# A decoder layer on one Trainium2 core: its forms of x at one place modulo 256 bytes

## Chip, core and metric

The chip is a Trainium2 (trn2). The kernel runs on one of its cores, and the metric is the device time of one execution in microseconds (us). A core has five engines that run their own instruction streams and wait for one another by semaphores: TensorE (PE), which multiplies a stationary operand, loaded first (PEld), with a moving one that streams past it; VectorE (DVE), ScalarE (ACT), GpSimd (POOL) and SyncE (SP), which here issues most DMAs. Operands lie in the on-chip memory SBUF, 128 partitions with byte addresses of their own; matmul results accumulate in PSUM.

## What is computed

One layer that joins two recurrent branches over 16 meta rows and 512 sequence rows of width 1024: retention (4 heads) and gated linear attention, "the linear branch" (4 heads). All arithmetic is float32.

```python
def hybrid_layer(h, norm_gain, w_in, w_gate_up, b_gate, ret_norm_gain, gla_norm_gain,
                 w_branch_ret, w_branch_gla, w_out):
    u = rms_norm(h, norm_gain)
    proj = u @ w_in
    (rq, rk, rv, rg, gq, gk, gv, gg, glr, m_ret, m_gla) = jnp.split(proj, points, axis=-1)
    ...
    o_ret = retention_chunked(rq, rk, rv)
    o_ret = head_group_norm(o_ret, ...) * jax.nn.silu(rg)
    ...
    o_gla = gla_chunked(gq, gk, gv, log_a)
    o_gla = head_rms_norm(o_gla, ...) * jax.nn.silu(gg)
    merged = jax.nn.sigmoid(m_ret) * (o_ret @ w_branch_ret) + jax.nn.sigmoid(m_gla) * (o_gla @ w_branch_gla)
    return h + merged @ w_out
```

The output is the final RMS norm of the 512 sequence rows.

## The kernel before

**Numbers in two parts.** A float32 operand is kept as hi + lo, both in the type fp32r: ACT casts hi, DVE subtracts it to give lo (`split`, L154, for weights; `form`, L684 to L690, for x). A product of two operands is three matmuls: hi by hi, hi by lo, lo by hi (`mm3` at L189, L192 and L193, and L318).

**Block products.** Most projections are done by `quad` (L257 to L396). It takes a 2x2 block matrix of x (two halves of the rows by two halves of the 1024 columns of the input, transposed) and a block of 2x256 weight columns, and needs seven block products instead of eight, on seven *forms*: the blocks A11, A12 and A22 and the combinations S1 to S4 of blocks. The order is A11 (product 1), A12 (2), S2 (6), S3 (7), S1 (5), A22 (4), S4 (3), or with `early` 1, 7, 6, 2, 5, 4, 3. One product (`product`, L302 to L319) is 2 column tiles by 4 k-blocks by 3 matmuls: 24 matmuls of a 128x128 stationary tile and 256 moving columns. With `wide` (gqk, rqk: queries and keys) the moving side has 264 columns, except for S1 and S4, where it has 256. With `rows=True` (gg, gv, rg, rv: gates and values of the linear branch and of retention; wo1: a part of the output projection) the form is stationary and the weight moves. Otherwise (gqk, rqk; mr, mg: merge gates; bg: projection of the linear branch) the weight is stationary and the form moves. The number behind a name is that of the head or pair of heads. The tiles gg_a, gg_b, gg_c and so on are a quad's three PSUM results.

**Weights.** They are loaded by SP (some with an addition on POOL's DMA), combined on DVE (L355, L356, L372, L379), split (`prepare`) into rotating buffers of hi and lo, and used by one product each. TensorE waits for the lo part where DVE is late.

**Forms.** Those of x are made at the start, from u00, u01 and u11 (parts of the normalised, transposed x), and read by all quads over w_in; the four blocks also by gq0, gk0 and gv0, which use no combinations (L428, L643). The linear branch has its own forms of its output for bg, and the merged rows (mh, ml, with their combinations ms, `merged_sums` L1471) have theirs for wo1; the last 256 columns of the output projection (`wo_p`, "wo2") use the merged rows directly, as stationary operands. Each form is a tile of 4 k-blocks; the stride between k-blocks follows from its width.

**Order.** The stages are generators that `weave` mixes: forget gates (L731 on) and first projections; gg0 with the linear attention; gqk1, gv1, gg1; bg0 and bg1; per head of retention rqk, rg, rv with scores and attention; mg and mr beside the attention of head 3 (`ret_attention`, L1329); the retention's branch product (br); wo. A scheduler of the framework then sets the row of instructions on each engine. A tile with an earlier tile's tag takes its place, and its first writer waits for the last reader of the earlier one. `quad` yields after each product, so that others' small matmuls come between products; `sooner` (gg0 only) prepares the weights of product 6 during product 2. `total` (L826) adds a product's result to the copy of another (gg_x, L334) into gsg, the gate's sum. At L910 to L954 stand small matmuls of the linear attention.

**Tiles in question.** xh0, xl0, xh1, xl1 hold the blocks of x (hi and lo by column half); fh3 to fh6 and fl3 to fl6 hold S1 to S4. o3 (oh, ol of head 3) takes the tags of xh0 and xl0; the first merged rows take xh1 and xl1, and their sums the tags of S1 to S4.

```python
        def product(i, form, w, ps, fresh, ready=None):
            ...
                    u = [row(f[form], kk)[:, col] if rows else row(f[form], kk)[:, :n] for f in forms]
                    v = [f[:, kk, :] if rows else f[:, kk, col] for f in (hi, lo)]
```

Of the kernel before, what the change touches and what calls it, by code (L numbers as in the profile page):

```python
# [21 lines left out]
F32 = mybir.dt.float32  # L22
F32R = mybir.dt.float32r
# [5 lines left out]
P = 128  # L29
D = 1024  # L30
T = 512
NM = 16
TT = T + NM
HT = TT // 2
HM = NM // 2
HW = 272
KD = D // P
NTB = T // P
# [3 lines left out]
C_GQ, C_GK, C_GV, C_GG = 6144, 6656, 7168, 8192  # L42
# [6 lines left out]
A11, A12, A22, S1, S2, S3, S4 = range(7)  # L49
# [59 lines left out]
def hybrid_kernel(ctx: ExitStack, tc: tile.TileContext, I, out: bass.AP):  # L109
    nc = tc.nc  # L110

    cp = ctx.enter_context(tc.tile_pool(name="cp", bufs=1))
# [13 lines left out]
    nc.gpsimd.memset(one, 1.0)  # L126


    xh = [cp.tile([P, 4, 2, HW], F32R, tag=f"xh{i}", name=f"xh{i}") for i in range(2)]
    xl = [cp.tile([P, 4, 2, HW], F32R, tag=f"xl{i}", name=f"xl{i}") for i in range(2)]  # L130
    ah = {(th, kh): xh[kh][:, :, th] for th in range(2) for kh in range(2)}
    al = {(th, kh): xl[kh][:, :, th] for th in range(2) for kh in range(2)}
    fh = [ah[0, 0], ah[0, 1], ah[1, 1]]
    fl = [al[0, 0], al[0, 1], al[1, 1]]
    fh += [cp.tile([P, 4, HW], F32R, tag=f"fh{i}", name=f"fh{i}") for i in range(3, 7)]
    fl += [cp.tile([P, 4, HW], F32R, tag=f"fl{i}", name=f"fl{i}") for i in range(3, 7)]

    rt = cp.tile([P, NTB + 1], F32, name="rt")
    rneg = cp.tile([P, NTB + 1], F32, name="rneg")
# [25 lines left out]
    def act(ins):  # L165
        return queue("act", ins)

    def vec(ins):
        return queue("vec", ins)
# [34 lines left out]
    def weave(dense, chain, skip=0):  # L204

        for n, _ in enumerate(dense):
            tick()
            if n >= skip:
                next(chain, None)
        for _ in chain:  # L210
            pass
# [286 lines left out]
    def meta_rows(psm, name):  # L498
# [9 lines left out]
    xc = ctx.enter_context(tc.tile_pool(name="xc", bufs=2))  # L508
    gctx = ctx.enter_context(ExitStack())
    g1 = gctx.enter_context(tc.tile_pool(name="g1", bufs=1))  # L510
    la = g1.tile([P, 5, 512], F32, name="la")
    gsum = g1.tile([P, 640], F32R, name="gsum")
    gsm = g1.tile([NM, NM], F32R, name="gsm")
    gmask = g1.tile([P, 3, P], I32, name="gmask")
# [8 lines left out]
    gp = gctx.enter_context(tc.tile_pool(name="gp", bufs=1, reuse_waits="tile"))  # L523
# [11 lines left out]
    ss = sp.tile([P, NTB + 1], F32, tag="ss5", name="ss5", bufs=1)  # L535


    xr = [gp.tile([P, D], F32, tag=("gq", "gk", "gX", "gX")[n], name=f"xr{n}", bufs=(1, 1, 2, 2)[n])
          for n in range(NTB)]
    xr.append(laf[:, :D])  # L540
# [3 lines left out]
    for q in range(4):  # L544
        raw = wraw(f"gv0_{q}_w", (P, 2, 512))
        for s in (slice(0, 1), slice(1, 2)) if q < 2 else (slice(0, 2),):
            k0, n = 2 * q + s.start, s.stop - s.start
            x = (nc.sync if k0 else nc.scalar).dma_start(u[k0 // 4][:, k0 % 4:k0 % 4 + n], I["xt"][:, k0:k0 + n])
# [57 lines left out]
    for q in range(4):  # L606
        raw = graw[q]
        hi, lo = wsplit([P, 2, 512], f"gv0_{q}")
        for kk in range(2):
            kh, k = divmod(2 * q + kk, 4)  # L610
# [3 lines left out]
            if k == kh == 0:  # L614
                nc.vector.tensor_copy(hi[:, kk, :], raw[:, kk, :])
                w = nc.vector.tensor_sub(lo[:, kk, :], raw[:, kk, :], hi[:, kk, :].bitcast(F32))
            x = nc.vector.scalar_tensor_tensor(xl[kh][:, k, :, :HT], u[kh][:, k], g, xh[kh][:, k, :, :HT].bitcast(F32),
                                               op0=ALU.mult, op1=ALU.subtract)
# [5 lines left out]
        if q == 3:  # L624
            for kh in range(2):
                for k in range(4):
                    x = nc.scalar.activation(u[kh][:, k], u[kh][:, k], AF.Copy, scale=ng[:, 4 * kh + k:4 * kh + k + 1])
# [54 lines left out]
    vec(nc.vector.scalar_tensor_tensor(u01, u00, -1.0, u01, op0=ALU.mult, op1=ALU.subtract))  # L682

    def form(i, x):  # L684
        act(nc.scalar.copy(fh[i][:, :, :HT], x))

        def rest():
            vec(nc.vector.tensor_sub(fl[i][:, :, :HT], x, fh[i][:, :, :HT].bitcast(F32)))

        return rest  # L690

    forms = [form(S1, u11)]
# [38 lines left out]
    def forget_gates():  # L731
# [22 lines left out]
        parts["gk0", 0] = wsplit([P, 4, 256], "gk0_0")  # L754
        forms.append(form(S2, u00))
        next_weights(0)
        forms.append(form(S4, u01))
        for i in (2, 0, 1, 3):
            forms[i]()
        yield  # L760
        def values(p):
# [78 lines left out]
    G = {}  # L840
# [3 lines left out]
                        lambda psm: meta_v(psm, p), False)  # L844

    def gla_g(p):
        sg = g1.tile([P, NTB, 512], F32, tag="gsg", name=f"gsg{p}")
        G["sg", p] = sg

        def evac(n, th, x, y):  # L850
            total(sg[:, 2 * th:2 * th + 2, n * 256:(n + 1) * 256], x, y)

        yield from quad((C_GG + p * 512, C_GG + p * 512 + 256), True, f"gg{p}", evac,
                        sooner=p == 0)

    def gla_qk(p):
        q = gp.tile([P, 2, T], F32, tag="gq", name=f"gq{p}")
# [404 lines left out]
        yield  # L1262

    def ret_g(h):
        sg = rp.tile([P, NTB, 512], F32, tag="sg", name=f"sg{h}")
        R["sg", h] = sg
        yield from quad((C_RG + h * 512, C_RG + h * 512 + 256), True, f"rg{h}", rows_into(sg, AF.Silu),
                        ahead=h % 3 == 0, behind=R.get(("pow", h - 1)))
# [60 lines left out]
    def ret_attention(h):  # L1329
        sh, sl, sm = R["s", h]  # L1330
        vh, vl = R["v", h]
        vm, sg = R["vm", h], R["sg", h]

        if h == 0:
            nc.gpsimd.memset(rp.tile([P, 16], F32, name="gap"), 0.0)
        oh, ol = [(rp if h < 3 else cp).tile([P, 4, T], F32R, tag=f"o{n}" if h < 3 else f"x{n}0", name=f"o{n}{h}")
                  for n in "hl"]
        R["o", h] = oh, ol

        def values(ib):  # L1340
            ps = pat(f"av{h}{ib}")
            for jb in range(ib + 1):
                o = SOFF[jb] + (ib - jb) * P
                mm3(ps, sh[:, o:o + P], sl[:, o:o + P], vh[:, jb, :], vl[:, jb, :], jb == 0, False)
            nc.tensor.matmul(ps, sm[:, ib * P:(ib + 1) * P], vm, start=False, stop=True)
            b6 = sp.tile([P, 6], F32, tag="b6", name=f"b6{h}{ib}")
            mv = sp.tile([P, 2], F32, tag="mv", name=f"mv{h}{ib}")
            nc.vector.bn_stats(b6, ps)
            nc.vector.bn_aggr(mv, b6)
            r = rstd_of(mv[:, 1:2], 1.0, P, f"g{h}{ib}")  # L1350
            nm = sp.tile([P, 1], F32, tag="nm", name=f"nm{h}{ib}")
            nc.vector.scalar_tensor_tensor(nm, mv[:, 0:1], -1.0, r, op0=ALU.mult, op1=ALU.mult)  # L1352
            on = tmp(f"on{h}{ib}")
            nc.scalar.activation(on, ps, AF.Identity, scale=r, bias=nm)  # L1354
            nc.vector.tensor_mul(sg[:, ib, :], on, sg[:, ib, :])

        for ib in range(NTB):
            values(ib)
            R["pow", h] = R["pow"]
            yield  # L1360
        if h < 2:
            yield
        for half in range(2):
            turn(sg, half, oh, ol, rgain, h * 4, f"ot{h}")
            yield
# [82 lines left out]
    for h in range(4):  # L1448
# [10 lines left out]
        else:  # L1459
            weave(run(ret_g(h), ret_v(h)), run(every(ret_rope(h), 3, 2, at if h else None), ret_scores(h)))  # L1460
    weave(gates_ret(), ret_attention(3))

    mh, ml = [[cp.tile([P, 4, T], F32R, tag=f"x{n}1", name=f"m{n}0"),
               rp.tile([P, 4, T], F32R, tag=("sg", "vl")[n == "l"], name=f"m{n}1")] for n in "hl"]
    sums = [[cp.tile([P, 4, 256], F32R, tag=f"f{n}{i}", name=f"ms{n}{i}") for i in range(3, 7)] for n in "hl"]
    mforms = [[m[0][:, :, :256], m[1][:, :, :256], m[1][:, :, 256:], *x] for m, x in zip((mh, ml), sums)]

    def merged(k, t):
        return [m[k // 4][:, k % 4, t * P:(t + 1) * P] for m in (mh, ml)]
# [30 lines left out]
    def residual():  # L1500
        nc.sync.dma_start(hs[0], I["x"][:, :512].rearrange("(t p) d -> p t d", p=P))
        yield
        nc.sync.dma_start(fgb, I["final_norm_gain"].to_broadcast([P, D]))
        nc.sync.dma_start(hs[1], I["x"][:, 512:].rearrange("(t p) d -> p t d", p=P))

    weave(ret_branches(), residual(), skip=14)

# [104 lines left out]
```

## Time and profile before

| what | us |
|---|---|
| median of 3 runs (lowest to highest) | 758.31 (757.18 to 758.43) |
| the profiled execution's own time | 759.11 |
| its span in the profile | 757.3 |
| granted TensorE clock over the span | 0.998 |
| DMA traffic over the span | 153 GB/s |

The 40 slices of the profile (tenths of a slice in which TensorE is busy) are 9 in all but the last. A row of the *chain of waits* has a start, a time and what the chain was on; the row of `x24` matmuls is one product. In the *timeline* a row has in addition the operation, the output, the inputs and their shapes. In the table of *windows* each engine's busy time has its instructions behind it in brackets. Busy time of one matmul (0.28 us and so on) is a modelled length that overlaps with the next one's; the step from one to the next is read from the chain's rows or from two starts.

### The profile page before, as it was taken

The numbers are of one execution on the slowest core, as the hardware profiler recorded it, in microseconds if no ns is written. First come the engines' busy times: TensorE is split into PE (matmuls) and PEld (weight loads), VectorE is DVE, ScalarE is ACT, GpSimd is POOL, SyncE is SP. The second block draws the span as 40 slices with busy tenths as digits, with TensorE's granted clock in tenths as the row PEclk, the third lists the DMA queues.
The fourth block names the chain that finished last, engine by engine and source line by source line (L and its number), as shares of the span: only waits on it lengthen the run. The fifth ranks groups of instructions, "written<-read, shape, count | busy, mean of one in ns | idle before, by whom it ended". The sixth has DMA issues, their size and how long they took to land.

```text
span 757.3 us, 14065 instructions
## 1 busy us (share of the span) xinstructions
PE 748.2 (99%) x5595; PEld 701.3 (93%) x5595; DVE 609.2 (80%) x873; ACT 450.4 (59%) x764; POOL 138.8 (18%) x173
## 2 busy tenths in 40 slices
PE   9999999999999999999999999999999999999996
PEld 6799899999999999999989999989999999988996
DVE  6699877679897789789957688966787989775994
ACT  7897584666974466556546555646464756532562
POOL 2211110101221122110530100440011210111142
PEclk9999999999999999999999999999999999999999
DMA  9863421821589972733783562795476356687503
GB/s 301 286 141 78 118 63 50 195 85 57 130 182 272 305 165 88 168 112 133 199 249 117 120 159 86 204 223 136 130 166 145 107 144 189 227 194 210 128 29 112
DMA packets 100138, 117.42 MB, mean 155 GB/s; under 512 B 5732, under 2 KB 90852, under 8 KB 99816
## 3 DMA queue, kind: packets, MB, share of 16 engines
q1 hardware_dynamic: 79896, 88.19, 36.7%
q0 software_dynamic: 19888, 27.79, 20.3%
q8 instruction: 44, 0.72, 0.4%
q10 hardware_dynamic: 288, 0.53, 0.2%
q14 instruction: 22, 0.18, 0.1%
HBM read 104.44 MB, written 11.53 MB: 153 GB/s over the span
## 4 chain that ended last, share of the span: by engine, by line
PE 86%; DVE 6%; ACT 2%; DMA 2%; issue 2%; POOL 1%; POOLq 0%; DVEq 0%; ACTq 0%
PE rqk_b L318 6%; PE rv_b L318 6%; PE rg_b L318 6%; PE rqk_c L318 5%; PE br_p L193 3%; PE br_p L189 3%; PE br_p L192 3%; PE gg_b L318 3%; PE gv_p L643 3%; PE mg_b L318 3%; PE rv_c L318 3%; PE rg_c L318 3%; PE mr_b L318 2%; PE bg_b L318 2%; PE gg_c L318 2%
## 5 line engine op out<-in xcount | busy, mean ns | idle before, releaser
L189 PE MATMUL br_p<-oh,br_h 128*128 128x512 f32 x128 | 50.0, 390 | 0.0
L193 PE MATMUL br_p<-oh,br_l 128*128 128x512 f32 x128 | 50.0, 390 | 0.0
L192 PE MATMUL br_p<-ol,br_h 128*128 128x512 f32 x128 | 49.8, 389 | 0.0
L154 ACT CAST rv_h<-rv_w 128x1024 fp32r<-128x1024 f32 x24 | 25.3, 1052 | 27.2 <-DVE rv_w L372 9.6
L154 DVE TENSOR_TENSOR rv_l<-rv_w,rv_h 128x1024 fp32r<-128x1024 f32 x24 | 29.3, 1221 | 9.2 <-ACT rv_h L154 9.2
L154 DVE TENSOR_TENSOR rg_l<-rg_w,rg_h 128x1024 fp32r<-128x1024 f32 x20 | 24.4, 1220 | 8.3 <-ACT rg_h L154 8.3
L154 ACT CAST rg_h<-rg_w 128x1024 fp32r<-128x1024 f32 x20 | 21.0, 1052 | 15.6 <-PE br_p L192 6.0
L282 POOL DMA_DIRECT2D rqk_x<-in_w_in_dram x8 | 10.4, 1302 | 105.4 <-DVE rv_l L154 80.6
L193 PEld LDWEIGHTS br_p<-oh,br_l 128*128 128x128 f32 x128 | 24.0, 188 | 5.2
L192 PEld LDWEIGHTS br_p<-ol,br_h 128*128 128x128 f32 x128 | 24.0, 188 | 4.7
L189 PEld LDWEIGHTS br_p<-oh,br_h 128*128 128x128 f32 x128 | 24.1, 188 | 4.5
L154 ACT CAST rqk_h<-rqk_w 128x1024 fp32r<-128x1024 f32 x20 | 21.1, 1053 | 11.5 <-PE rqk_c L318 2.9
L154 ACT CAST br_h<-br_w 128x1024 fp32r<-128x1024 f32 x16 | 16.8, 1050 | 18.7 <-PE br_p L192 9.5
L154 DVE TENSOR_TENSOR rqk_l<-rqk_w,rqk_h 128x1024 fp32r<-128x1024 f32 x20 | 24.4, 1221 | 3.9 <-ACT rqk_h L154 3.8
L1354 ACT ACTIVATE on<-av,nm,g_r 128x512 f32<-128x512 f32 x16 | 12.5, 779 | 25.3 <-DVE nm L1352 25.3
L318 PE MATMUL rv_b<-rv_l,fh 128*128 128x256 f32 x96 | 27.1, 282 | 0.2 <-DVE rv_l L154 0.2
L318 PE MATMUL rqk_b<-fh,rqk_h 128*128 128x256 f32 (+1 forms) x96 | 27.2, 283 | 0.0
L318 PE MATMUL rqk_b<-fh,rqk_l 128*128 128x256 f32 (+1 forms) x96 | 27.1, 282 | 0.0
L318 PE MATMUL rqk_b<-fl,rqk_h 128*128 128x256 f32 (+1 forms) x96 | 27.1, 282 | 0.0
L318 PE MATMUL rg_b<-rg_h,fl 128*128 128x256 f32 x96 | 27.0, 281 | 0.0
L318 PE MATMUL rv_b<-rv_h,fl 128*128 128x256 f32 x96 | 27.0, 281 | 0.0
L318 PE MATMUL rg_b<-rg_l,fh 128*128 128x256 f32 x96 | 26.9, 280 | 0.0
(721 smaller groups left out, 3260.8 us busy)
## 6 DMA issues: line engine op xcount, KB each, us to landing
rv_w<-in_w_in_dram SPq DMA_DIRECT2D x16, 512.0 KB, 4.2
br_w<-in_w_branch_ret_dram SPq DMA_DIRECT2D x16, 512.0 KB, 3.4
rqk_w<-in_w_in_dram SPq DMA_DIRECT2D x12, 512.0 KB, 4.8
rg_w<-in_w_in_dram SPq DMA_DIRECT2D x12, 512.0 KB, 4.5
rqk_x<-in_w_in_dram SPq DMA_DIRECT2D x8, 512.0 KB, 4.0
rqk_x<-in_w_in_dram POOLq DMA_DIRECT2D x8, 512.0 KB, 8.0
rg_x<-in_w_in_dram SPq DMA_DIRECT2D x8, 512.0 KB, 3.7
rg_x<-in_w_in_dram POOLq DMA_DIRECT2D x8, 512.0 KB, 7.8
```

The costliest lines, as they stand in the source:

```text
L154: return nc.scalar.copy(hi, src), nc.vector.tensor_sub(lo, src, hi.bitcast(F32))
L189: m = nc.tensor.matmul(o, lh, rh, start=first, stop=False)
L192: nc.tensor.matmul(o, lh, rl, start=False, stop=False)
L193: m = nc.tensor.matmul(o, ll, rh, start=False, stop=last)
L282: x = nc.gpsimd.dma_start(t, block(0, 1), accum_op=ALU.add)
L318: m = nc.tensor.matmul(ps[t][:, :n] if wide else ps[t], l, r, start=first and j == 0, stop=kk == 3 and j == 2, skip_group_check=not fresh ...
L643: m = nc.tensor.matmul(pss[t], (al if j == 1 else ah)[t // 2, kh][:, k, c], (lo if j == 2 else hi)[:, kk, :], start=q == kk == j == 0, sto ...
L1354: nc.scalar.activation(on, ps, AF.Identity, scale=r, bias=nm)
```

## The change

The tiles of x and its sums become six: x0, x1 and x2, hi and lo, with 576, 896 and 640 columns per k-block, so that the stride between k-blocks is 2304, 3584 and 2560 bytes, multiples of 256. Unused tiles (`gap`) of 16, 32 or 48 floats shift what follows them in its pool. S1 and S4 keep 256 columns instead of 264. S4 takes the place of a part of the block A(1,0) (second half of the rows, first half of the columns), which no form uses, but which gq0, gk0 and gv0 read; its making moves from the forget gates into `gla_g(0)`, behind the first product of gg0, and the tile sg of that stage is allocated behind it. o3 takes the place of S2 and S3 (x2). Of the sums of merged rows, S1's lies behind the first merged rows in x1, S2's and S3's take x0, and S4's takes o3's place.

Addresses that follow from the allocation, modulo 256 bytes, by k-block where they change:

| operand | before | after |
|---|---|---|
| A11, A12 of x, hi and lo | 192 and 64 in turn | 128 |
| A22 of x | 0 and 128 in turn | 128 |
| S1 to S4 of x | 192, 0, 64, 128 | 128 |
| A(1,0) of x | 0 and 128 in turn | 192 |
| linear branch: A11 | 64 | 128 |
| linear branch: A22 | 0 | 128 |
| linear branch: S3 | hi 0, lo 128 | 128 |
| linear branch: A12, S1, S2, S4 | 128 | 128 |
| merged rows, first half of the columns | 192 | 128 |
| merged rows, second half | hi 64, lo 128 | 128 |
| sums of merged rows | 192 | 128 |
| split weights, hi and lo | 192 | 192 |

The diff, with most unchanged lines left out:

```diff
-    xh = [cp.tile([P, 4, 2, HW], F32R, tag=f"xh{i}", name=f"xh{i}") for i in range(2)]
-    xl = [cp.tile([P, 4, 2, HW], F32R, tag=f"xl{i}", name=f"xl{i}") for i in range(2)]
+    def gap(pool, n, name):
+        pool.tile([P, n], F32, name=name)
+
+    gap(cp, 48, "gap0")
+    x0, x1, x2 = [[cp.tile([P, 4, w], F32R, tag=f"x{n}{i}", name=f"x{n}{i}") for n in "hl"]
+                  for i, w in enumerate((576, 896, 640))]
+    gap(cp, 16, "gap1")
+
+    def halves(t, w):
+        return t[:, :, :2 * w].rearrange("p k (t c) -> p k t c", t=2)
+
+    xh, xl = [[halves(a, HW), halves(b, 320)] for a, b in zip(x0, x1)]
     ah = {(th, kh): xh[kh][:, :, th] for th in range(2) for kh in range(2)}
     al = {(th, kh): xl[kh][:, :, th] for th in range(2) for kh in range(2)}
-    fh = [ah[0, 0], ah[0, 1], ah[1, 1]]
-    fl = [al[0, 0], al[0, 1], al[1, 1]]
-    fh += [cp.tile([P, 4, HW], F32R, tag=f"fh{i}", name=f"fh{i}") for i in range(3, 7)]
-    fl += [cp.tile([P, 4, HW], F32R, tag=f"fl{i}", name=f"fl{i}") for i in range(3, 7)]
+    fh, fl = [[a[0, 0], a[0, 1], a[1, 1], b[:, :, 640:], c[:, :, :320], c[:, :, 320:], z[:, :, 320:]]
+              for a, z, b, c in zip((ah, al), x0, x1, x2)]
...
     g1 = gctx.enter_context(tc.tile_pool(name="g1", bufs=1))
+    gap(g1, 16, "gap2")
     la = g1.tile([P, 5, 512], F32, name="la")
+    gap(g1, 48, "gap3")
     gsum = g1.tile([P, 640], F32R, name="gsum")
...
+    gap(gp, 32, "gap4")
     xr = [gp.tile([P, D], F32, tag=("gq", "gk", "gX", "gX")[n], name=f"xr{n}", bufs=(1, 1, 2, 2)[n])
...
     def form(i, x):
-        act(nc.scalar.copy(fh[i][:, :, :HT], x))
+        w = 256 if i in (S1, S4) else HT
+        h, l, x = fh[i][:, :, :w], fl[i][:, :, :w], x[:, :, :w]
+        act(nc.scalar.copy(h, x))
         def rest():
-            vec(nc.vector.tensor_sub(fl[i][:, :, :HT], x, fh[i][:, :, :HT].bitcast(F32)))
+            vec(nc.vector.tensor_sub(l, x, h.bitcast(F32)))
...
         next_weights(0)
-        forms.append(form(S4, u01))
-        for i in (2, 0, 1, 3):
+        for i in (2, 0, 1):
             forms[i]()
...
     def gla_g(p):
+        def evac(n, th, x, y):
+            total(sg[:, 2 * th:2 * th + 2, n * 256:(n + 1) * 256], x, y)
+
+        products = quad((C_GG + p * 512, C_GG + p * 512 + 256), True, f"gg{p}", evac, sooner=p == 0)
+        if p == 0:
+            next(products)
+            form(S4, u01)()
+            yield
         sg = g1.tile([P, NTB, 512], F32, tag="gsg", name=f"gsg{p}")
         G["sg", p] = sg
-
-        def evac(n, th, x, y):
-            total(sg[:, 2 * th:2 * th + 2, n * 256:(n + 1) * 256], x, y)
-
-        yield from quad((C_GG + p * 512, C_GG + p * 512 + 256), True, f"gg{p}", evac,
-                        sooner=p == 0)
+        yield from products
...
     def ret_g(h):
+        if h == 0:
+            gap(rp, 16, "gap5")
         sg = rp.tile([P, NTB, 512], F32, tag="sg", name=f"sg{h}")
+        if h == 0:
+            gap(rp, 48, "gap6")
         R["sg", h] = sg
...
         if h == 0:
-            nc.gpsimd.memset(rp.tile([P, 16], F32, name="gap"), 0.0)
-        oh, ol = [(rp if h < 3 else cp).tile([P, 4, T], F32R, tag=f"o{n}" if h < 3 else f"x{n}0", name=f"o{n}{h}")
-                  for n in "hl"]
+            gap(rp, 16, "gap7")
+        if h < 3:
+            oh, ol = [rp.tile([P, 4, T], F32R, tag=f"o{n}", name=f"o{n}{h}") for n in "hl"]
+        else:
+            oh, ol = [cp.tile([P, 2560], F32R, tag=f"x{n}2", name=f"o{n}{h}")[:, 16:16 + 4 * T]
+                      .rearrange("p (k c) -> p k c", k=4) for n in "hl"]
         R["o", h] = oh, ol
...
-    mh, ml = [[cp.tile([P, 4, T], F32R, tag=f"x{n}1", name=f"m{n}0"),
-               rp.tile([P, 4, T], F32R, tag=("sg", "vl")[n == "l"], name=f"m{n}1")] for n in "hl"]
-    sums = [[cp.tile([P, 4, 256], F32R, tag=f"f{n}{i}", name=f"ms{n}{i}") for i in range(3, 7)] for n in "hl"]
-    mforms = [[m[0][:, :, :256], m[1][:, :, :256], m[1][:, :, 256:], *x] for m, x in zip((mh, ml), sums)]
+    def rows4(t, o, c):
+        return t[:, o:o + 4 * c].rearrange("p (k c) -> p k c", k=4)
+
+    m0 = [cp.tile([P, 3584], F32R, tag=f"x{n}1", name=f"m{n}0") for n in "hl"]
+    mh, ml = [[rows4(t, 0, T), rp.tile([P, 4, T], F32R, tag=("sg", "vl")[n == "l"], name=f"m{n}1")] for n, t in zip("hl", m0)]
...
     weave(ret_branches(), residual(), skip=14)
+
+    mforms = []
+    for n, m, t in zip("hl", (mh, ml), m0):
+        s23 = cp.tile([P, 2048], F32R, tag=f"x{n}0", name=f"ms{n}0")
+        s4 = cp.tile([P, 1024], F32R, tag=f"x{n}2", name=f"ms{n}2")
+        mforms.append([m[0][:, :, :256], m[1][:, :, :256], m[1][:, :, 256:], rows4(t, 4 * T, 256),
+                       rows4(s23, 0, 256), rows4(s23, 1024, 256), rows4(s4, 0, 256)])
```

On DVE at the start of gg0 the rows stand as follows; xl is S4's lo part, gk_p a product of keys, gg_6_h and gg_6_l the split weights of product 6. Before:

```order
L868 TENSOR_TENSOR gk_441<-gk_p_589,rb 128x264
L868 TENSOR_TENSOR gk_441<-gk_p_591,rb 128x264
L372 TENSOR_TENSOR gg_w_732<-gg_w_732,gg_x_734 128x1024
L379 TENSOR_TENSOR gg_w_733<-gg_w_733,gg_w_732 128x1024
L154 TENSOR_TENSOR gg_6_l<-gg_w_732,gg_6_h 128x1024
L826 TENSOR_TENSOR gsg_731<-gg_a,gg_x_775 128x2x256
L923 TENSOR_TENSOR gK_823<-gX_812,gk_441 128x512
```

And on DVE at the same place of the changed program:

```order
L883 TENSOR_TENSOR gk_440<-gk_p_586,rb 128x264
L883 TENSOR_TENSOR gk_440<-gk_p_588,rb 128x264
L701 TENSOR_TENSOR xl_82<-u_130,xh_81 128x4x256
L380 TENSOR_TENSOR gg_w_728<-gg_w_728,gg_x_730 128x1024
L838 TENSOR_TENSOR gsg_775<-gg_a,gg_x_771 128x2x256
L387 TENSOR_TENSOR gg_w_729<-gg_w_729,gg_w_728 128x1024
L162 TENSOR_TENSOR gg_6_l<-gg_w_728,gg_6_h 128x1024
L938 TENSOR_TENSOR gK_822<-gX_811,gk_440 128x512
```

S4's subtraction has come in ahead of the weights' sums, and the add into gsg now stands ahead of the second weight sum and of gg_6_l, where it stood behind both.

On DVE at the forget gates, where the four combinations were subtracted; fl are the lo parts. Before:

```order
L154 TENSOR_TENSOR gk_0_l<-gk_w_468,gk_0_h 128x1024
L688 TENSOR_TENSOR fl_89<-u_130,fh_85 128x4x264
L688 TENSOR_TENSOR fl_88<-u_131,fh_84 128x4x264
L688 TENSOR_TENSOR fl_90<-u_130,fh_86 128x4x264
L688 TENSOR_TENSOR fl_91<-u_131,fh_87 128x4x264
L791 SCALAR_TENSOR_TENSOR fg_a<-fg_a,fg_e_510 128x512
```

And at the same place of the changed program, where xl are the lo parts:

```order
L162 TENSOR_TENSOR gk_0_l<-gk_w_467,gk_0_h 128x1024
L701 TENSOR_TENSOR xl_86<-u_129,xh_85 128x4x264
L701 TENSOR_TENSOR xl_84<-u_130,xh_83 128x4x256
L701 TENSOR_TENSOR xl_86<-u_129,xh_85 128x4x264
L803 SCALAR_TENSOR_TENSOR fg_a<-fg_a,fg_e_507 128x512
```

Three are left; one of them has 256 columns for 264.

## Prediction

> **What bounds the kernel now.** I read three things in this order: the shares of the page, the chain of work that ended last, and the chain's own rows, where each stretch of 24 matmuls of one product (one `product` call, 128 stationary columns by 256 or 264 moving ones) is one row: start, us, line, count.
>
> ```profile
> span 757.3 us, 14065 instructions
> PE 748.2 (99%) x5595; PEld 701.3 (93%) x5595; DVE 609.2 (80%) x873; ACT 450.4 (59%) x764; POOL 138.8 (18%) x173
> PE 86%; DVE 6%; ACT 2%; DMA 2%; issue 2%; POOL 1%; POOLq 0%; DVEq 0%; ACTq 0%
> ```
>
> The chain is TensorE's for 86%, so a shorter step from one matmul to the next shortens the span nearly everywhere. The next view is the chain from 237 to 294 us, three kinds of block product one behind the other:
>
> ```profile
> 237.12 2.82 PE bg_c L318 x24
> 242.68 2.72 PE bg_a L318 x24
> 245.40 2.72 PE bg_b L318 x24
> 248.12 2.83 PE bg_c L318 x24
> 250.94 2.73 PE bg_b L318 x24
> 253.67 2.93 PE rqk_b L318 x24
> 265.33 2.85 PE rqk_b L318 x24
> 268.18 2.90 PE rqk_c L318 x24
> 273.92 2.85 PE rg_b L318 x24
> 285.30 2.84 PE rg_b L318 x24
> 288.14 2.75 PE rg_c L318 x24
> 290.89 2.85 PE rg_b L318 x24
> ```
>
> All but the two rqk rows of 2.93 and 2.90 (264 columns) are 24 matmuls of 128x256 without a wait. They take 2.72 to 2.85 us, 113 to 119 ns each. What differs is where the operands lie (table in the section on the change). In bg (branch product of the linear branch) the weight is stationary, at 192 modulo 256 bytes in every row; the form moves. The A12, S1 and S4 products (242.68, 245.40, 250.94), with a form constantly at 128, go at 2.72 or 2.73. S3 (237.12), hi at 0 and lo at 128, takes 2.82; A22 (248.12), constantly at 0, takes 2.83. In rg the form is stationary and the weight moves. Forms whose place changes from one k-block to the next take 2.84 or 2.85; A22 (288.14), which alternates between 0 and 128, takes 2.75. So I read the time as one of place: about 2.73 where the form is at 128 against a weight at 192, about 0.1 more elsewhere.
>
> **The change part by part.** (1) *Forms of x to one place.* Nothing is added per product; 24 matmuls stay 24. rg: the seven products of rg0 run from 273.92 to 290.89+2.85 = 293.74, 19.82 us. At 2.73 each they take 19.11: 0.7 per quad. For constant stationary forms at 128 no row exists. The nearest are the A22 row above, half of whose blocks lie at 128 (2.75), and from the other side the slowest row of this shape, of wo1 (2.88, below). I take 2.73 and keep 2.88 for a rival. rqk: its weight is stationary and the seven products run from 253.67 to 273.92, 20.25 us. The two of 256 columns (S1, S4: 265.33 is one) go from 2.85 to 2.73. For five of 264 at a constant place no row exists; between 2.90 (no gain) and 2.73x264/256 = 2.81 I take 2.84. New sum 2x2.73+5x2.84 = 19.66: 0.59 per quad. The merge gates also move the form:
>
> ```profile
> 648.37 2.84 PE mr_c L318 x24
> 654.18 2.84 PE mr_b L318 x24
> ```
>
> 7x(2.82-2.73) = 0.63 per quad, with 2.82 taken as the mean since other rows of mr stand at 2.80. Where TensorE ends last throughout the quad I count it whole: rg0 to rg2 and rv0 to rv2 6x0.7 = 4.2; mg0, mg1 1.26; mr1 0.63; rqk0 to rqk3 2.36; gqk1 0.59 (taken as rqk); gv1 and gg1 1.4. Of gg0 the last five products 0.5, of rv3 the last five 0.5. Nothing from 187 to 231 us, where a load of og and the vector work after it end last. Together 11.44.
>
> (2) *Linear branch's input.* The three rows above 2.73 of bg1 (A11 taken as A22, S3, A22): 3x0.1 = 0.3, estimated from the rows 237.12 and 248.12. bg0 lies before 237 and gets none.
>
> (3) *Merged rows and their sums.* The last rows of the chain, and two matmuls of the last projection with 42 steps between them:
>
> ```profile
> 734.30 2.80 PE wo_c L318 x24
> 737.10 2.88 PE wo_b L318 x24
> 739.81 0.28 PE L189 MATMUL wo_p<-wo_h,mh 128*128 128x256 f32 x1
> 744.78 0.28 PE L189 MATMUL wo_p<-wo_h,mh 128*128 128x256 f32 x1
> ```
>
> 737.10 is S4 of wo1: form stationary, constantly at 192, as the weight is; 2.88, or 120.0 ns each, the slowest rhythm of this shape. 734.30 is A22, at 64 (hi) and 128 (lo): 2.80. Behind them 42 steps take 4.97 us, 118.3 ns, so 72 of them have 72x5 ns = 0.36 over 113.3. At one place of 128 I count 0.3 for the last three products of wo1 and 0.4 for the rest. Sum of (1) to (3): 12.4.
>
> (4) *S4's form moved.* S4 now lies in x's A(1,0), which gq0, gk0 and gv0 still read, so its cast on ACT and subtraction on DVE move from the forget gates to a point inside gg0.
>
> ```profile
> 40.87 2.85 PE gq_p L428 x24
> 61.71 2.86 PE gg_a L318 x24
> 64.57 0.12 PE ge L910
> 65.74 2.86 PE gg_b L318 x24
> 41.21 4.76 DVE L688 TENSOR_TENSOR fl<-u,fh 128x1056 fp32r<-128x1056 f32 x4
> 63.21 1.23 DVE L379 TENSOR_TENSOR gg_w<-gg_w,gg_w 128x1024 f32<-128x1024 f32 x1
> 64.36 1.22 DVE L154 TENSOR_TENSOR gg_l<-gg_w,gg_h 128x1024 fp32r<-128x1024 f32 x1
> 65.49 0.68 DVE L826 TENSOR_TENSOR gsg<-gg_a,gg_x 128x512 f32<-128x512 f32 x1
> ```
>
> The four subtractions take 4.76, 1.19 each; DVE does the same work in all, at another time. But its order changes: the add into gsg, which waits for the end of product 2 (64.57), stood behind gg_l, the low weights of product 6, and now stands ahead of it. Queued behind it on DVE are the 1.23 and 1.22 above; for gg_l TensorE waits. From the end of gg_a to product 6 it was 65.74-64.57 = 1.17, filled by small products. Now it is at least 0.62 (to the next start) + 1.15 + 1.22 = 3.0: 1.8 lost. Against it stand the products from 34 to 64, ten groups of 24 at 0.13 at most (2.86-2.73), 1.3, which nothing else counts. Net 0.5 lost. ACT's cast delays the copy gg_x, which has from 61.71 to 64.57 to be ready: nothing.
>
> (5) *256 columns for S1 and S4*: 8 of 264 columns of four instructions of about 1.2, 0.15 in all, on engines that wait here; the products read 256 before. Nothing.
>
> (6) *o3 in S2's and S3's place, sums of merged rows in three others.* S2 and S3 are last read by mr1's products before 651.21 (648.37+2.84); o3's first write comes later:
>
> ```profile
> 659.14 0.83 ACT L494 ACTIVATE oh<-ot,rgain 128x256 fp32r<-128x256 f32 x2
> 725.99 1.22 ACT L154 CAST msh<-sigr 128x512 fp32r<-128x512 f32 x2 [2.20 <-DVE sigr L1491]
> ```
>
> 8 us of cover. The sum that takes o3's place is the last of the four, written around 726, after the branch products have read o3. If this cover went, the wait would be a part of a product, under 3 us; I count nothing. The memset removed on POOL (18% busy) costs nobody.
>
> (7) *Given back.* In the rows between products and small matmuls the fast rhythm may have to be found again: for some fourteen interruptions between 300 and 664 I take 0.1 each, 1.4, the gain of one product each, an estimate from 2.83-2.73. And DVE is the next bound:
>
> ```profile
> 273.00:295.00 22.00, 22.00 (x203) 21.35 (x205) 22.00 (x29) 16.02 (x24) 8.21 (x4) 1.00 0.37 106
> 586.00:609.00 23.00, 23.00 (x211) 22.26 (x213) 23.00 (x32) 15.95 (x27) 4.93 (x5) 1.00 0.37 115
> 705.00:731.00 26.00, 25.81 (x207) 25.10 (x205) 26.00 (x37) 14.89 (x30) 7.88 (x9) 1.00 0.25 69
> 614.42 1.15 DVE rv_l L154
> 615.62 2.98 PE rv_b L318 x23
> ```
>
> Columns: PE, weight loads, DVE, ACT, POOL busy, clock, DMA share, GB/s. DVE is full to the last 0.01 us in all three. From 586 to 609 and from 705 to 731 the chain goes over to DVE and a faster TensorE only waits longer (rv3's product 6 starts at 615.62 behind rv_l), so rg3, rv3's first two and wo1's first four count for nothing. From 273 to 295 DVE also has work that can wait; I take 1.0 lost there and in rv0 to rv2, between 0 and the 2.1 that rg0 to rg2 bring.
>
> Sum: 12.4-0.5-1.4-1.0 = **9.5 us** off the profiled run's own 759.11 gives 749.6. The shown runs' median, 758.31, lies 0.8 below that run: **748.8**.
>
> [...]
>
> **The rivals.** *(a) Only moving forms gain.* The A22 rows of rg may owe their 2.75 to alternation, not to 128. Then rg, rv, gv1, gg1, gg0 and wo keep their time: of the 12.4 go 4.2+1.4+0.5+0.5+0.7 = 7.3; 5.1 stays, less 0.5 and about half of (7), 1.2: 3.4, **754.9**. For it: no row shows a constant stationary form that is fast. Against it: the 2.88 of S4 in wo1 shows that a stationary form's place matters.
>
> *(b) DVE takes more.* All of 2.1 in rg0 to rg2 and the same in rv0 to rv2 goes to DVE: 4.2 lost instead of 1.0, gain 6.3, **752.0**. Against it: in rg0 the chain stays with TensorE although DVE is full.
>
> *(c) Place does nothing, or the rows' differences come from the data or the order.* Then of the change only (4) is left, between 0.5 (with cover that I don't see) and its full 1.8, midway 1.2: **759.5**. For it, that only one kernel was seen; against it, that bg's rows return to 2.72 wherever the place is 128.
>
> *(d) Slower.* A stationary form at one constant place locks in the slow rhythm, whichever place: S4 of wo1, the only row here with hi and lo constantly at one place, shows 2.88. Ten row quads (rg0 to rg2, rv0 to rv2, gv1, gg1 and most of gg0 and rv3) at 7x2.88 = 20.16 against 19.82 lose 3.4; with (4) without its offset 1.8 and the column products' gain of 5.1 lost to longer waits only in part (2.5 left), 2.7 more than before: **761.0**. It decides when the row products come out above 2.83. For it: that row. Against it: there weight and form share 192, here they don't, and A22 of wo1 (734.30), constant with hi at 64 and lo at 128, takes 2.80.
>
> **How the numbers follow.** Forecast 0.62, (a) 0.17, (b) 0.08, (c) 0.06, (d) 0.07. The forecast's own range: the fast end has nothing of (7) and of (4), 264 columns at 2.81 (25 products at 0.03, 0.75), and also gains 0.1 in each of the thirteen products that I left at nothing under DVE (rg3, two of rv3, four of wo1): 12.4+0.75+1.3 = 14.4, 743.9. Its other end is (b). The range reaches from 744.0 over (a) to 757.0, beyond which lie most of (c) and (d). A measurement of this kernel tells about 0.2%, 1.5 us, from no change. Faster by more: forecast, (a), (b), less a little: 0.85. Within: most of (c) and the ends of (a) and (d): 0.08. Slower by more: (d) and the bad end of (c): 0.07.
>
> **What would show it.** Right: rg and rv rows of 2.72 to 2.75 for all seven products; bg c rows at 2.72; rqk at 2.81 to 2.87 and 2.73; wo_b at 2.73; a gap of about 3 us between gg_a and the next gg_b. Wrong: row products still at 2.84 (a) or above 2.86 (d); the chain going to DVE from 273 to 345 (b); TensorE waiting for o3 or for the merged sums; bg rows as before (c).

## The result, and the profile after

| | median of its runs, us | lowest to highest | ratio to before | 95% interval |
|---|---|---|---|---|
| before | 757.89 (22 runs) | 756.84 to 758.79, one run at 810.82 | | |
| the change | 759.70 (22 runs) | 756.75 to 762.16 | 1.0023 | 1.0013 to 1.0032 |

The change makes the kernel slower by a little; forecast were 748.8 us, with a range of 744 to 757. The runs of the change also spread over 5.4 us, those of before over 2.0 (the one at 810.82 apart). The profiled execution of the change took 760.18 us of its own, with a granted clock of 0.994. Its page:

```profile
span 758.4 us, 14064 instructions
PE 746.5 (98%) x5595; PEld 699.4 (92%) x5595; DVE 608.8 (80%) x873; ACT 450.1 (59%) x764; POOL 138.6 (18%) x172
PE 85%; DVE 7%; ACT 3%; issue 2%; DMA 2%; POOL 1%; POOLq 0%; DVEq 0%; ACTq 0%
```

TensorE's share of the chain is one point lower than before, DVE's and ACT's are one point higher each (rounded). Where that happens is seen by following the same row of work through both chains. gqk_c is the first product of gqk1 that runs without a break. Here are gg0's first matmul (from the timeline) and the row of gqk_c (from the chain), before and, in the second fence, after:

```profile
58.71 0.28 PE L318 MATMUL gg_b<-gg_h,xh 128*128 128x256 f32 x1
106.41 2.92 PE gqk_c L318 x24
```

```profile
57.45 0.28 PE L326 MATMUL gg_b<-gg_h,xh 128*128 128x256 f32 x1
110.51 2.88 PE gqk_c L326 x24
```

The change is 4.1 us late there, although gg0's first matmul started 1.3 us earlier than before. Later it makes good 3.0 of the 4.1: its span is only 758.4-757.3 = 1.1 longer. So there are two questions: what costs 4.1+1.3 = 5.4 us from gg0's start to gqk_c, and why do the 650 us behind it bring 3 and not some 9. For the first, the windows after, then before (us; PE, weight loads, DVE, ACT, POOL busy; granted clock; DMA share; GB/s):

```profile
64.00:66.00 2.00, 0.67 (x4) 0.29 (x2) 2.00 (x3) 1.35 (x3) 0.00 (x0) 1.00 0.00 0
66.00:68.00 2.00, 0.60 (x3) 0.46 (x3) 2.00 (x3) 2.00 (x7) 1.02 (x2) 0.66 0.00 0
68.00:70.00 2.00, 2.00 (x11) 2.00 (x11) 2.00 (x5) 1.48 (x2) 0.00 (x0) 0.50 0.69 196
70.00:72.00 2.00, 2.00 (x12) 2.00 (x11) 1.35 (x2) 0.00 (x0) 0.43 (x1) 0.50 0.19 67
```

```profile
64.00:66.00 2.00, 2.00 (x17) 1.96 (x17) 2.00 (x3) 2.00 (x6) 0.19 (x1) 1.00 0.00 0
66.00:68.00 2.00, 2.00 (x20) 2.00 (x19) 2.00 (x5) 2.00 (x6) 0.45 (x1) 1.00 0.61 175
```

TensorE idles for 2.7 of 4 us while DVE is full, and behind that its granted clock is 0.50: 11 and 12 matmuls in 2 us, where 17 and 20 ran before. The timeline shows what the 2.7 us wait for, the first two matmuls of product 6 (in brackets the idle time before and what ended it):

```profile
65.75 0.39 PE L326 MATMUL gg_b<-gg_h,xh 128*128 128x256 f32 x1 [1.33 <-ACT gg_h L162]
67.54 0.58 PE L326 MATMUL gg_b<-gg_l,xh 128*128 128x256 f32 x1 [1.40 <-DVE gg_l L162]
```

For the second question, rows of the chain after:

```profile
251.38 2.83 PE bg_c L326 x24
254.20 2.83 PE bg_b L326 x24
...
268.56 2.75 PE rqk_b L326 x24
271.30 2.91 PE rqk_c L326 x24
...
276.95 2.72 PE rg_b L326 x24
293.27 2.72 PE rg_b L326 x24
...
300.89 2.83 PE rv_a L326 x24
735.40 2.83 PE wo_c L326 x24
738.23 2.83 PE wo_b L326 x24
```

In all these products the form is at 128 and the weight at 192; rqk_c has 264 columns, the others 256. There are two times for this one shape: 2.72 or 2.83, with little between (2.75 where a product changes over). I call them two *rhythms*: steps of about 113 and 118 ns that hold over a stretch. rg0 is at 2.72 from its first product to its last, rv0 behind it at 2.83, bg1 at 2.83 where it had four rows of 2.72 to 2.74 before.

### The profile page after: what moved, and what is told of

It reads as the page before. It is cut to its first block, busy times and chain, and to the rows that moved or that the text cites. A ratio compares the mean times of both kernels' runs of the same rounds, so it can differ in the third digit from the quotient of the medians.

```text
span 758.4 us, 14064 instructions
## 1 busy us (share of the span) xinstructions
PE 746.5 (98%) x5595; PEld 699.4 (92%) x5595; DVE 608.8 (80%) x873; ACT 450.1 (59%) x764; POOL 138.6 (18%) x172
## 4 chain that ended last, share of the span: by engine, by line
PE 85%; DVE 7%; ACT 3%; issue 2%; DMA 2%; POOL 1%; POOLq 0%; DVEq 0%; ACTq 0%
PE rqk_b L326 6%; PE rv_b L326 6%; PE rg_b L326 6%; PE rqk_c L326 5%; PE br_p L201 3%; PE br_p L200 3%; PE br_p L197 3%; PE gg_b L326 3%; PE mg_b L326 3%; PE rv_c L326 3%; PE gv_p L654 3%; PE rg_c L326 3%; PE bg_b L326 2%; PE mr_b L326 2%; PE gg_c L326 2%
## 5 line engine op out<-in xcount | busy, mean ns | idle before, releaser
L326 PE MATMUL rqk_b<-xh,rqk_h 128*128 128x264 f32 (+1 forms) x128 | 36.3, 283 | 0.0
L326 PE MATMUL rv_b<-rv_l,xh 128*128 128x256 f32 x128 | 35.8, 279 | 0.4 <-DVE rv_l L162 0.4
L326 PE MATMUL rv_b<-rv_h,xh 128*128 128x256 f32 x128 | 36.1, 282 | 0.0
L326 PE MATMUL rqk_b<-xh,rqk_l 128*128 128x264 f32 (+1 forms) x128 | 36.1, 282 | 0.0
L326 PE MATMUL rqk_b<-xl,rqk_h 128*128 128x264 f32 (+1 forms) x128 | 36.1, 282 | 0.0
L326 PE MATMUL rv_b<-rv_h,xl 128*128 128x256 f32 x128 | 35.7, 279 | 0.0
L326 PE MATMUL rg_b<-rg_h,xh 128*128 128x256 f32 x128 | 35.6, 278 | 0.0
L326 PE MATMUL rg_b<-rg_l,xh 128*128 128x256 f32 x128 | 35.6, 278 | 0.0
L326 PE MATMUL rg_b<-rg_h,xl 128*128 128x256 f32 x128 | 35.6, 278 | 0.0
```

Of the source, the lines that this page charges most:

```text
L326: m = nc.tensor.matmul(ps[t][:, :n] if wide else ps[t], l, r, start=first and j == 0, stop=kk == 3 and j == 2, skip_group_check=not fresh ...
```

## The experiments

The comparison with before is each time with runs on the same chip.

**s4_unblocked.** S4's cast goes ahead of ACT's table load (the load belongs to `pad`'s Exp, which moves behind the cast), and the add into gsg behind gg_6_l:

```diff
-        act(nc.scalar.activation(pad[:, 1:2], one, AF.Exp))
         yield
...
+            m = total(sg[:, 2 * th:2 * th + 2, n * 256:(n + 1) * 256], x, y)
+            if p == n == th == 0:
+                after(m, low[1])
...
             next(products)
-            form(S4, u01)()
+            rest = form(S4, u01)
+            act(nc.scalar.activation(pad[:, 1:2], one, AF.Exp))
+            rest()
```

> The changed kernel with S4's cast put ahead of ACT's table load and the add into gsg put behind gg_6_l on DVE; places as changed. Theory A (the loss sits in gg0: wait for gg_6_l, then a lower granted clock): in the profile of the change the stretch from the end of gg_a (63.11) to product 3's first full row (78.48) is 15.4 us, before it was 9.7 (64.57 to 74.24); 5.7 come back, about 754.0 by the median, clock 1.00 from 60 to 80 us, no gap of over 0.5 us ahead of product 6. Rival B (that gap is made good later, what failed is only the gain of the places): 759 to 760 as the change.

Measured: 755.85 us (10 runs, 755.24 to 757.16), ratio to before 0.9976 [0.9967, 0.9986]; the clock is 1.00 from 57 to 80 us. gg0's first matmul, the second one of product 6, and gqk_c:

```profile
57.86 0.28 PE L326 MATMUL gg_b<-gg_h,xh 128*128 128x256 f32 x1
65.97 0.39 PE L326 MATMUL gg_b<-gg_l,xh 128*128 128x256 f32 x1 [0.93 <-DVE gg_l L162]
106.77 2.88 PE gqk_c L326 x24
```

gqk_c is 3.7 us earlier than in the change. Theory A holds in kind: the median comes back by some 3.5 of the expected 5.7 (0.9976 against 1.0023 of about 757.7). One reason is that not every execution of the change loses its clock: over its 22 runs the granted clock goes from 0.991 to 1.000. The other is that the gap is not closed. 0.93 us of idle time stay, where 0.5 at most was expected, and from gg0's first matmul to gqk_c it is 106.77-57.86 = 48.9 us, where it was 47.7 before. So the 1.8 us that this kernel gains on before is the gain of the places less some 1.2 in gg0: about 3 us, an estimate from these rows, and not 10.

**fill.** 28 matmuls of no use ahead of product 6 of gg0, the wait left as it is:

```diff
+            if sooner:
+                pf = ppt(f"{name}_fill")
+                for i in range(28):
+                    m = nc.tensor.matmul(pf[:, :256], fh[A11][:, 0, :P], fh[A12][:, 0, :256], start=True, stop=True)
+                    if i == 0:
+                        pin(m)
+                order[:] = [m]
             product(6, S2, w11, b, False, ready)
```

> The changed kernel with 28 matmuls of no use (3.3 us) on TensorE in the gap ahead of product 6 of gg0; the wait for gg_6_l stays. If the granted clock falls because TensorE idles: clock 1.00 from 64 to 76 us, product 6 still starts at about 67.7, but the stretch behind it takes 8.5 us as before instead of 10.9, so 2.3 less than the change, about 757.4, and a narrower spread of its runs. If the clock falls for another reason (load on ACT and DVE, chance): 0.5 to 0.8 in that stretch as in the change, about 759.7.

Measured: 758.80 us (11 runs, 757.22 to 759.57), 1.0014 [1.0005, 1.0022]. The chain and its row of gqk_c:

```profile
64.89 3.35 PE gg_fill L387 x28
68.24 2.83 PE gg_b L326 x24
...
108.83 2.88 PE gqk_c L326 x24
```

The clock is 1.00 in every window from 57 to 80. Product 6 starts 0.7 later than in the change (68.24 against 67.54), of which 0.5 arose ahead of gg0 (its first matmul starts at 57.92 against 57.45), and it takes 2.83. From gg0's first matmul to gqk_c it is 50.9 us, in the change 53.1. With the wait left in and only the idle time filled, the clock stays: over the 11 executions it was granted at 0.997 to 1.000, where 12 of the 22 of the change lie under 0.997. So the idle time of TensorE is a condition of the fall here. The time came out 1.4 above the expectation, and by the medians alone (1.0014 against 1.0023, with intervals that overlap) the gain isn't clear: not every execution of the change is slowed, so its median had less to give back. The spread fell from 5.4 to 2.4 us, as expected.

**cast_first, gsg_behind, after_again.** The two edits of s4_unblocked one at a time, and the change itself beside them.

> The changed kernel with only one of the two edits of s4_unblocked: S4's cast ahead of ACT's table load; the add into gsg still ahead of gg_6_l on DVE. In the change's profile the cast starts at 61.20 behind the table load (59.79, 1.28) and DVE waits 1.43 for it. If the wait ahead of product 6 comes mainly from that: S4's subtraction starts about 1.4 earlier, product 6 about 1.4 earlier than 67.54, the idle time of TensorE falls below 2 us, the clock stays at 1.00, and 3 to 4 of the 5.7 come back: 756.5. If it comes mainly from the order of gsg (the prediction's reason): under 1 us comes back, 759.

> The other of the two edits alone: gsg behind gg_6_l on DVE, S4's cast still behind the table load. If the table load is the main cause, gg_6_l can start only about 65.8 (S4's subtraction 62.26, then the two sums), 0.5 to 1.2 earlier than in the change: product 6 at about 66.9, clock still down in most executions, 758.5. If the order of gsg is the main cause: product 6 at 65.8, clock 1.00, 756.5.

> The changed kernel beside the two others on one chip: 759 to 760.5, granted clock under 0.997 in more than half of its executions, 0.5 to 0.7 for some microseconds behind 66 us.

Measured: 757.36, 0.9995 [0.9983, 1.0007]; 758.56, 1.0011 [0.9998, 1.0023]; 758.69, 1.0018 [1.0006, 1.0030] (10 runs each). What blocks what is read from the timeline; first of the change:

```profile
59.79 1.28 ACT L831 ACT_TABLE_LOAD   x1
61.20 1.03 ACT L698 CAST xh<-u 128x1024 fp32r<-128x1024 f32 x1
62.26 1.22 DVE L701 TENSOR_TENSOR xl<-u,xh 128x1024 fp32r<-128x1024 f32 x1 [1.43 <-ACT xh L698]
64.54 0.68 DVE L838 TENSOR_TENSOR gsg<-gg_a,gg_x 128x512 f32<-128x512 f32 x1
66.27 1.22 DVE L162 TENSOR_TENSOR gg_l<-gg_w,gg_h 128x1024 fp32r<-128x1024 f32 x1
```

Then of cast_first, and of gsg_behind:

```profile
60.92 1.23 DVE L701 TENSOR_TENSOR xl<-u,xh 128x1024 fp32r<-128x1024 f32 x1
65.27 1.22 DVE L162 TENSOR_TENSOR gg_l<-gg_w,gg_h 128x1024 fp32r<-128x1024 f32 x1
```

```profile
65.67 1.22 DVE L162 TENSOR_TENSOR gg_l<-gg_w,gg_h 128x1024 fp32r<-128x1024 f32 x1
```

gg_l starts at 64.36 before, at 66.27 in the change, 1.0 earlier with the cast first, 0.6 earlier with gsg behind, at 64.69 with both. TensorE's idle time ahead of product 6 is 2.73 in the change, 1.74 in cast_first, 2.25 in gsg_behind and 0.93 with both; before, it had none there. So the cast behind the table load is the larger of two causes, gsg is the smaller, and 0.93 stays with both edits. Still on DVE ahead of gg_l, and not there before, is S4's subtraction itself (1.22). No run leaves it out, so it isn't shown that it makes the 0.93. The medians follow: cast_first gets back 1.3 us of after_again, gsg_behind no more than the noise.

Both kernels still lost their clock in their profiles (cast_first 0.50 from 68 to 70, gsg_behind 0.60 from 66 to 68). For gsg_behind that was expected if the table load is the main cause, and product 6 (66.94 for 66.9) and the time came out as expected too; for cast_first the expected return of the clock was wrong, and 0.9 us of the time with it. In these three profiles the clock is at 0.50 for 6.83 us in the change (66.64 to 73.47) and for 3.41 us in cast_first (67.01 to 70.42) and gsg_behind (66.40 to 69.81). In the 3.41 us ahead of the fall TensorE was busy for 1.58, 1.67 and 1.70 us.

after_again missed its expectation: its median lies below 759, and two of its ten executions, not more than half, had a granted clock under 0.997. The profiled one kept its clock through the same idle time:

```profile
57.14 0.28 PE L326 MATMUL gg_b<-gg_h,xh 128*128 128x256 f32 x1
66.00:68.00 2.00, 0.78 (x6) 0.78 (x7) 2.00 (x4) 2.00 (x6) 0.75 (x2) 1.00 0.00 0
68.00:70.00 2.00, 2.00 (x19) 2.00 (x17) 2.00 (x5) 1.16 (x2) 0.00 (x0) 1.00 0.80 220
...
107.73 2.88 PE gqk_c L326 x24
```

The same program, the same wait, the clock at 1.00, and gqk_c at 107.73 and not 110.51. Of these 2.8 us, 0.3 were there when gg0 started (57.14 against 57.45), so the clock alone is 2.5 us; the span is 756.0 against 758.4. The remaining 5.4-2.5 = 2.9 is the wait.

**bench_places.** No part of the layer, only products as in the kernel, with both places under control.

```diff
+    for mo in (0, 64, 128, 192):
+        for so in (0, 64, 128, 192):
+            for w in (32, 64, 96, 128, 192, 256, 384, 512):
+                m = nc.tensor.matmul(pi[:, :w], isx, iv[:, :w], start=True, stop=True)
...
```

> Leaves the whole layer out: only groups of 24 matmuls of 128x256 (products as in the kernel, hi and lo, eight k-blocks and column tiles), for each of 16 pairs of places (moving at 0, 64, 128, 192 modulo 256 bytes, stationary at 0, 64, 128, 192), eight groups each, ahead of each group one other matmul of 32 to 512 columns. Theory P (place decides alone): one step per pair whatever stands ahead: 113 ns at moving 128 with stationary 192, 118 at 0 with 192, 120 at 192 with 192. Rival Q (two rhythms, and what stands ahead decides which): at 128 with 192 some of the eight groups go at 113 and others at 118, and within a group the step stays. Also to be read: whether any pair always goes at 113.

Measured (406.23 us, one run): the mean step of the second half of each group, from the starts in the trace, put together by the difference of the two places:

```
stationary less moving   pairs x groups   step, ns
  0                      4 x 8            120.0 in all 32
 64                      4 x 8            113.3 or 113.4 in 18, 117.7 or 117.8 in 14
128                      4 x 8            118.3 to 120.0
192                      4 x 8            117.7 or 117.8 in all 32
```

Neither P nor Q alone: in this bench the *difference* of the places decides which rhythms there are (four pairs with one difference read alike), and at 64 bytes, and only there, there are two. Each group differs from the other seven of its pair in what stands ahead of it; which of the two a given matmul ahead brings is not the same in all four pairs. A group keeps its rhythm from its second half on to its end: at 64 no mean lies between 113.4 and 117.7.

**rows_apart and cols_apart.** In the change and in s4_unblocked, column products (moving form at 128, stationary weight at 192) stand at +64, row products (moving weight at 192, stationary form at 128) at -64, which is 192. The row products' weights are put at 64; the mirror does the opposite.

```diff
-            hi, lo = wsplit([P, 4, 256], f"{name}_{i}")
+            hi, lo = wsplit([P, 4, 256], f"{name}_{i}", 32 if rows else 0)
...
-        w = wsplit([P, 4, 256], f"wo{o}_{kh}")
+        w = wsplit([P, 4, 256], f"wo{o}_{kh}", 32)
```

Here 32 is an offset in floats inside a buffer that is 64 floats longer; in cols_apart the two cases of the first line are exchanged, and the second has 0.

> s4_unblocked with the split weights of the row products (gg, gv1, rg, rv, wo) at 64 modulo 256 and not at 192, forms at 128 as before it; instruction order unchanged. Theory D (what decides is the stationary place less the moving one modulo 256: at +64 both rhythms occur, at -64 only 118 ns, as bench_places showed for eight groups each): the row products go from -64 to +64 and enter the fast rhythm in about half of their stretches; their mean step falls from 116.9 to about 115.5, 700 triples, about 3 us, about 753. Rival E (the bench's difference is chance, in the kernel the row products at -64 were at 113 in whole quads): the step stays at 116.5 to 117 and the time at 755.9.

> The mirror of rows_apart: weights of the row products back at 192, those of the column products of 256 and 264 columns in the block products at 64, so that both kinds stand at -64 (stationary less moving). Theory D: the column products lose their 113 ns too (108 of 430 triples in the change's profile), mean step 117.5 to 118, some 0.5 to 1.5 us slower than s4_unblocked, 756.4 to 757.4. Rival E: no difference from s4_unblocked and from rows_apart.

Measured: rows_apart 752.58 us (5 runs, 751.61 to 754.14), 0.9941 [0.9928, 0.9955]; cols_apart 757.83 (11 runs), 1.0002 [0.9992, 1.0011]. Counted from the starts in the profiles' traces, in threes of matmuls (hi by hi, hi by lo, lo by hi) that run without a gap; fast is under 115.6 ns a step:

```
                 columns, 256 wide       rows, 256 wide
                 fast of    mean ns      fast of    mean ns
before            56 of 430   117.7      112 of 702   117.9
the change       108 of 430   116.7      141 of 695   116.9
s4_unblocked     177 of 430   116.0      111 of 701   117.1
rows_apart       178 of 430   116.0      362 of 701   115.5
cols_apart        38 of 430   117.5       56 of 701   117.4
```

Theory D gave 115.5 ns and 753 for rows_apart, and 756.4 to 757.4 for cols_apart, which came 0.4 above that. Its "at -64 only 118 ns" does not hold in the kernel: 111 row threes of s4_unblocked and 56 of cols_apart are fast at -64. Rival E falls all the same: with the same instructions in the same order, 128 bytes in the place of the weights are worth 0.9976-0.9941 of about 757.5, 2.7 us. rows_apart's chain: the first row of rg0, which takes 2.72 in the change (all seven of rg0 are now at 2.83), two rows of rv0 and the last two of wo1, which take 2.83 in the change:

```profile
270.56 2.83 PE rg_b L327 x24
...
295.13 2.72 PE rv_a L327 x24
297.85 2.72 PE rv_b L327 x24
...
727.46 2.72 PE wo_c L327 x24
730.18 2.72 PE wo_b L327 x24
```

So a single stretch can go either way; the sum is what falls. The kernel beats both before and the change.

**bench_fine.** The same with 16-byte steps, and with 264 columns.

> Leaves the whole layer out: groups of 24 matmuls with moving operands at 0 and stationary ones at 0 to 240 modulo 256 in steps of 16 bytes for 256 columns, and in steps of 32 for 264 columns, eight different matmuls ahead. Theory D: at 0 120.0 ns, at 64 both 113.4 and 117.8, at 128 118.5, at 192 117.8, as in bench_places; places between lie between, and whether one of them is always fast is to be read. For 264 columns: two rhythms at +64, the slow 120.0 that the kernel shows and, if the gain is 4.5 ns there too, a fast one of about 117. Rival F (each length has its own rhythm, places count for little at 264): 120 to 121 at all places.

Measured (601.35 us, one run), mean steps as above:

```
256 wide, stationary less moving   0: 120.0   64: 113.3 to 113.4 (6 of 8), 117.7 and 117.8   192: 117.7 to 117.8
                                   208: 116.6 to 116.9   all other places: 116.5 to 122.7
264 wide                           64: 120.0 in all 8    all other places: 119.7 to 126.7
```

At 256 columns no place is always fast, and none but 64 ever is. The fast rhythm of 117 at 264 columns, which theory D allowed, does not exist at any place tried; neither does F hold, as places reach from 119.7 to 126.7.

## Why the prediction was wrong

**The step that failed first** is in (1): "I take 2.73 and keep 2.88 for a rival", and behind it the reading "about 2.73 where the form is at 128 against a weight at 192". The rows of bg on which it rested were right, but they were one rhythm of two, seen in one stretch. Place permits 2.72, it does not bring it. In the change 108 of 430 column threes and 141 of 695 row threes have it, where the sum took every product that DVE doesn't hold up. By the table the mean steps fell by 1.0 ns for columns and for rows, which is 430x3 and some 700x3 steps, 3.4 us in all (an estimate), where the sum had 12.4 and another 1.3 ahead of 64 us. rg0 came out as forecast (276.95 to 295.99, 19.04 for 19.11), but by luck, as the next paragraph shows, and what follows it did not.

**Rows and columns were taken as one case.** The form's place was read as "128", but the bench shows the difference with its sign. Row products at -64 are at 117.7 or 117.8 in all 32 groups of the bench; in the kernel some run fast, in whole stretches: rg0 follows on rqk0's last product, at 2.75 from 274.21, without a gap. (In cols_apart that product takes 2.82, and rg0 2.83 throughout.) The A22 row of 2.75 was read as half gained because half its blocks lie at 128; by the bench it is the other half, at 0 against a weight at 192, that stands at 64. Rival (a), only moving forms gain, had that side right, but column products gain in part only, so even its 754.9, with 5.1 us from the places and little lost in gg0, was too good: s4_unblocked, with most of gg0's loss taken out, has 755.85.

**Column products of 264.** Forecast 2.84; the rows are 2.88 to 2.93 still, and the bench shows 120.0 ns (2.88) as the step at +64. That part of the term (five of seven products) was nearly nothing: the mean step went from 121.5 to 121.1 ns.

**(2)** can't be read from the change's profile, in which bg1 fell into the slow rhythm (above): in s4_unblocked, with the same places, six rows of bg1 are at 2.72, S3 and A22 among them, as (2) said:

```profile
236.08 2.72 PE bg_c L326 x24
246.96 2.72 PE bg_c L326 x24
```

**(3)**: S4 of wo1 went from 2.88 to 2.83, as equal places (120.0 in the bench) were given up, but A22 went from 2.80 to 2.83.

**(4)** is the second step that failed, and it made the change slower instead of faster. It was right in mechanism and too small. It forecast 1.8 us of wait, less 1.3 gained ahead of it. The gain ahead was 1.3 (57.45 against 58.71); the loss 5.4. The row that the sum lacked is ACT's table load of 1.28 us: "ACT's cast delays the copy gg_x ... nothing" looked behind the cast, not at what stands ahead of it. DVE idled 1.43 for the cast, and from the end of product 2 (63.11) to the matmul that needs gg_l (67.54) it became 4.4 where the sum had 3.0. By gqk_c this wait had cost 2.9. The 2.5 us of clock behind it the prediction did not have at all. The granted clock was 0.50 for 6.83 us in the profile of the change and 1.00 from 57 to 76 us in that of after_again, and in both TensorE was busy for 1.27 us from 64 to 68 us (0.67+0.60 and 0.49+0.78). In the change it was never idle there for more than 1.4 us at a time (1.33 and 1.40). Why the one execution lost its clock and the other kept it isn't shown by these runs.

**(6)** held: the last product of mr1 and of wo1 start 1.2 and 1.1 us later than before (662.81 against 661.58, 738.23 against 737.10), so nothing is lost between them to o3 or to the sums. **(5)** no run measures by itself. **(7)**, DVE as the next bound, was hardly put to the test, since TensorE did not get faster by enough.

**Rival (c)**, place does nothing, gave 759.5, close to what was measured, by another way: places do act. In the bench, groups at 113.3 and at 120.0 ns have the same shapes and loads, and differ in the two operands' places. What inside the chip makes the difference isn't shown by these runs. **Rival (d)** named the right sign and the wrong cause: no row product of the change stands at 2.88 for its place; the slow ones are at 2.83.

**What stays open**: what decides which of the two rhythms a stretch takes, at a difference of 64, and in the kernel's row products at -64 too. It isn't mere chance: the row products of rv1 and rv2, with the same work ahead, both turn fast at the same product (435.75 and 553.57 in the change's chain), and so does rv1 of s4_unblocked at 431.15. Nor is it fixed by the program: the last six products of bg1 go at 117.8 ns a step in the profile of the change and at 113.3 in that of after_again, the same code.

## What to carry to other kernels

A duration that one row shows under a condition is not yet the effect of that condition: ask whether other rows with the same condition show it too, and, with two operands, vary both before one is moved. A stage of the kernel that holds work back for an engine's table load (1.28 us here) or queue should be read from what stands *ahead* of the moved instruction as well as from what stands behind it. The 2.73 us that TensorE idled here cost 2.5 us more in clock, and in only some executions (2 of the 10 of after_again and 12 of the 22 of the change have a granted clock under 0.997), so that a wider spread of the runs (5.4 us against 2.0) is itself a sign.

## What the runs showed that was not expected

With 128x256 matmuls in three-part products, as the bench has them, the step depends on the places of stationary and moving operand modulo 256 bytes through their difference: 120.0 ns at 0, 117.7 or 117.8 at 192, and 113.3 or 117.8, kept for whole stretches, at 64. In the kernel some stretches at 192 run at 113.3 too. With most of gg0's wait taken out and the difference of 64 given to row products as well, the kernel of the change becomes 0.59% (0.45 to 0.72) faster than before, at 752.58 us.
